# A decoder layer on one core: row factors spread over the partitions through DRAM in place of matmuls with ones, and the next half's work queued behind the residual adds

## The chip, the core and the metric

The kernel runs on one core of a Trainium2 chip. A core has a matrix engine (TensorE, here PE, with its weight loads as PEld), a vector engine (VectorE, DVE), an activation engine (ScalarE, ACT), a general engine (GpSimd, POOL) and a queue engine (SyncE, SP) that issues most transfers. Each runs its own list of instructions in order and waits on semaphores for the others. Tiles lie in an on-chip memory of 128 partitions; matmul results lie in banks of 128x512 f32. The metric is the device time of one execution in microseconds (us).

## What is computed

One layer of a decoder on 2048 tokens of width 1024, all in float32:

```python
xn = rms_norm(h, mix_norm_w)
q, f_logit, i_v, g, lru_x, lru_gate = split(xn @ w_in)      # 512 columns each
o_hg  = hgrn2_mix(q, f_logit, i_v, g, ...)   # gated linear recurrence, 4 heads, times silu(g)
o_lru = rglru_mix(lru_x, lru_gate, ...)      # conv, gates, linear recurrence, times gelu
h = h + concat(o_hg, o_lru) @ w_out
hn = rms_norm(h, ffn_norm_w)
h = h + (silu(gate) * up) @ w_down           # gate, up = split(hn @ w_gate_up)
return rms_norm(h, final_norm_w)

def rms_norm(x, w):
    return x * rsqrt(mean(x * x, axis=-1) + EPS) * w
```

What matters here is the first rms_norm: each token (a row of x) has one factor, rsqrt of its mean square.

## The kernel before

The tokens are worked on in two halves of 1024, each in two chunks of 512 (c = 0, 1) or eight row tiles of 128 (tt counts four of them in a chunk). A half goes through the input projection, the two mixers, the output projection, the FFN up and the FFN down. Every f32 matmul is done as three matmuls of split operands: a high part, rounded by ACT (L169 for weights, L233 for activations) or by a scaled copy, and a low part, the rest, subtracted by DVE (L170, L234). Names say which: whi_in and wlo_in are the input weights' parts, xn_c_00 and xn_c_01 the high parts of chunk c (first and last four of eight k slices), xn_c_10 and xn_c_11 the low parts.

**Row factors.** The Squares of x run on ACT with a sum along the row (L566 for half 0, L632 for half 1), DVE adds the parts (L558), POOL raises to the power -0.5 (L559). The result, ss_x, has a token's factor in a partition, 128 x 4 for a chunk. The projections of q, f and the rest need x with features in partitions and tokens along the row (tiles xk, 128 x 512), so the 512 factors must lie along the row, the same in all partitions. `row_spread` (L585) does this: for each of four row tiles DVE multiplies the identity by the factors (dgx, L590) and PE multiplies ones by it (tpbx, L591), which leaves the factors along the row in a bank. Half 0 multiplies xk by the bank (L598); half 1 copies the bank to a tile `row` on ACT (L639) and multiplies by that (L646).

In half 0 the first projection (v, `tok_wide`, L604) works on x without the factors and is scaled afterwards, in chunks pv_0 and pv_1; `row_spread` was called from its hook `between`, in the middle of its matmuls. Then come pa and pb (L261 to L263), which need xn.

**Half 1's preparation in half 0.** `norm_steps(c)` makes half 1's xn: `stat` (loads of x and the Squares), `spread`, and eight `apply` (load of xk, L646, the split). These steps are put into slots. `slot(i)` is called at eight places i = -4 to -1 of chunk 1's gate loop (after the Silu, L295, and the product with v, L1236) and at 28 places of the output projection's loop, after each residual add (L1303). Stats stand at slots -4 to 3, spreads at 8 and 9, applies at 12 to 27. In half 1 the same slots hold the FFN's first operands (act_a to act_g, from hn). A slot's code is only emitted there: the order on each engine is set by a scheduler that simulates a timeline and takes what it thinks is ready first. `tc.issue_after(ins)` adds an edge to that schedule: instructions emitted under it, on the engine of `ins`, come behind `ins`.

**The output projection** is seven products in the order p1, p2, p6, p5, p7, p3, p4 of sums of the mixers' outputs (operands mx_a to mx_g, made from hg, y and their sums s at L1224), into banks pox and poyp (L1298). DVE adds each bank to a tile res that holds x, and SP writes it to DRAM as h.

Of the kernel before, what the change touches and what calls it, by code (L numbers as in the profile page):

```python
# [8 lines left out]
F32 = mybir.dt.float32  # L9
F32R = mybir.dt.float32r  # L10
AF = mybir.ActivationFunctionType
ALU = mybir.AluOpType

P = 128
SEQ = 2048
D = 1024
KT = D // P
# [20 lines left out]
def hybrid_layer(ctx: ExitStack, tc: tile.TileContext, x, x_t, norm_w, cols, w_in, gate_w, w_out, w_gu, w_down, out):  # L38
# [26 lines left out]
    def late(nm):  # L65
        return sb.tile([P, CW], F32, tag="late", name=nm, bufs=5)
# [4 lines left out]
    def aux(nm):  # L71
        return psp.tile([P, CW], F32, tag="aux", name=nm)
# [25 lines left out]
    hst = const.tile([P, NU], F32, name="hst")  # L98
    nc.gpsimd.memset(hst, 0.0)
    v = nc.vector  # L100
    ones = const.tile([P, 1], F32, name="ones")
    nc.gpsimd.memset(ones, 1.0)
    tinies = const.tile([P, 17, 4], F32, name="tinies")
    n4 = [0]

# [456 lines left out]
    def row_factors(c, rows):  # L562
        sums = [small.tile([P, 4], F32, tag="ss", name=f"ss{n}_x0_{c}", bufs=8) for n in range(2)]
        for i, p in enumerate(rows):
            tt, n = divmod(i, 2)
            nc.scalar.activation(out=p, in_=p, func=AF.Square, scale=1.0 / 32.0, accum_out=sums[n][:, tt : tt + 1])  # L566
        return factor(sums, f"x0_{c}")
# [16 lines left out]

    def row_spread(c, rs, nm="x0"):  # L585
        nm = f"{nm}_{c}"
        pbc, dg = aux("tpb" + nm), late("dg" + nm)
        for tt in range(TPC):
            ts = slice(tt * P, (tt + 1) * P)
            v.tensor_scalar(out=dg[:, ts], in0=ident, scalar1=rs[:, tt : tt + 1], scalar2=None, op0=ALU.mult)  # L590
            nc.tensor.matmul(pbc[:, ts], lhsT=ones.broadcast_to([P, P]), rhs=dg[:, ts], start=True, stop=True)  # L591
        return pbc

    def normalised(c, xs, pbc):
        xn = act_tile(f"xn0_{c}")
# [5 lines left out]
                quarter.extend([ins, dve])  # L601
        return xn

    def tok_wide(w4, xt, nm, between):  # L604
        banks = [bank(f"{nm}_{tt}") for tt in range(TPC)]
        for k in range(KT):
            whi, wlo = w4[k // 2]
            ks = slice((k % 2) * CW, (k % 2 + 1) * CW)
            order = [(tt, i) for tt in range(TPC) for i in range(3)]
            if k == 0:  # L610
                order.sort(key=lambda o: (o[1], o[0]))
            for tt, i in order:
                w = (whi, whi, wlo)[i][:, ks]
                a = part(xt, int(i == 1), k, slice(tt * P, (tt + 1) * P))
                ins = nc.tensor.matmul(banks[tt], lhsT=a, rhs=w, start=(k + i == 0), stop=(k == KT - 1 and i == 2))  # L615
            if k in between:
                with tc.issue_after(ins.ins):
                    between[k]()
        return banks

    def norm_steps(c):
        box = {}
        sums = []

        def stat(tt):
            if tt == 0:
                sums.extend(small.tile([P, 4], F32, tag="ss", name=f"ss{n}_x1_{c}", bufs=8) for n in range(2))
            r0 = T + c * CW + tt * P
            for n in range(2):
                p = xin(f"x1_{c}_{tt}_{n}")  # L630
                nc.sync.dma_start(out=p, in_=x[r0 : r0 + P, n * CW : (n + 1) * CW])
                nc.scalar.activation(out=p, in_=p, func=AF.Square, scale=1.0 / 32.0, accum_out=sums[n][:, tt : tt + 1])  # L632
            if tt == TPC - 1:
                box["rs"] = factor(sums, f"x1_{c}")

        def spread():
            pbc = row_spread(c, box["rs"], "x1")
            box["row"] = late(f"row1_{c}")
            nc.scalar.copy(out=box["row"], in_=pbc)  # L639

        def apply(k):
            if k == 0:
                box["xn"] = act_tile(f"xn1_{c}")
            p = xin(f"xk1_{c}_{k}")
            nc.sync.dma_start(out=p, in_=x_t[k * P : (k + 1) * P, T + c * CW : T + (c + 1) * CW])
            v.scalar_tensor_tensor(  # L646
                out=p, in0=p, scalar=par[:, C_NW + k : C_NW + k + 1], in1=box["row"], op0=ALU.mult, op1=ALU.mult
            )
            split([part(box["xn"], s, k) for s in range(2)], p)

        return box, [lambda tt=tt: stat(tt) for tt in range(TPC)], spread, [lambda k=k: apply(k) for k in range(KT)]
# [442 lines left out]
    for half in range(2):  # L1094
# [12 lines left out]
        for c in range(NC):  # L1107
            if c == 0:
                wv = ws.take(4)
                vts = []  # L1110
            vt = block(f"v{half}_{c}", F32)
            vts.append(vt)
            if half == 0:
                def factors(c):
                    rows[c] = row_factors(c, acc[c])

                wide = []
                banks = tok_wide(wv, xw[c], f"pv0_{c}", {7 - 3 * c: lambda c=c: wide.append(row_spread(c, rs[c]))})
                for tt in range(TPC):
                    r = rs[c][:, tt : tt + 1]  # L1120
                    if tt % 2:
                        v.tensor_scalar(out=vt[:, tt, :], in0=banks[tt], scalar1=r, scalar2=None, op0=ALU.mult)
                    else:
                        nc.scalar.activation(out=vt[:, tt, :], in_=banks[tt], func=AF.Copy, scale=r)
                xt.append(normalised(c, xs[c], wide[0]))
                continue
            for tt in range(TPC):
                ps = tok_mm(wv, xt[c], tt, f"pv{half}_{c}_{tt}")
                nc.scalar.copy(out=vt[:, tt, :], in_=ps)
                later.pop(0)()  # L1130
# [80 lines left out]
        def slot(i):  # L1211
            for f_ in fill.pop(i, ()):
                f_()
# [13 lines left out]
        for c in range(NC):  # L1227
            for tt in range(TPC):
                ps = tok_mm(wg, xt[c], tt, f"pg{half}_{c}_{tt}")
                hook(32 + c * TPC + tt)  # L1230
                if lrus and (c, tt) == (0, 1):
                    exps()
                    ends()
                sg = page(f"sg{half}_{c}_{tt}")
                table_act(sg, ps, AF.Silu)
                v.tensor_tensor(out=vts[c][:, tt, :], in0=vts[c][:, tt, :], in1=sg, op=ALU.mult)  # L1236
                if c == 1:
                    slot(tt - 4)
            t = block(f"hg{half}_{c}", F32)
            hg.append(t)  # L1240
            for tt in range(TPC):
                tp = transposed(tt, 0, vts[c][:, tt, :], f"o{half}_{c}_{tt}")
                nc.scalar.activation(
                    out=t[:, :, tt * P : (tt + 1) * P], in_=tp, func=AF.Copy, scale=par[:, C_HN : C_HN + 1]
                )
            if c == 0:
                operand("p1", t)
                operand("p2", ys[0])
# [30 lines left out]
        for i, name in enumerate(OORDER):  # L1279
            wo = wos.take(2)  # L1280
            if i < 6:
                wos.ahead(2)
                prepare(OORDER[i + 1])
            if name in ("p2", "p5"):
                banks_y = [aux(f"poy{name}_{tt}_{half}") for tt in range(TPC)]
            banks = banks_y if name in ("p2", "p5", "p3") else banks_x
            first = name in ("p1", "p2", "p5")
            a = op.pop(name)
            c, n = to[name]
            if i in (1, 2, 5):  # L1290
                residual_in(*to[OORDER[i + 1]])
            for tt in range(TPC):
                tsl, ps = slice(tt * P, (tt + 1) * P), banks[tt]
                for q in range(4):
                    whi, wlo = (w[:, (q % 2) * CW : (q % 2 + 1) * CW] for w in wo[q // 2])
                    ahi, alo = (z[:, q, tsl] for z in a)
                    for m, (x_, y_) in enumerate(((ahi, whi), (ahi, wlo), (alo, whi))):
                        nc.tensor.matmul(  # L1298
                            ps, lhsT=x_, rhs=y_, start=first and q + m == 0, stop=q == 3 and m == 2, skip_group_check=not first
                        )  # L1300
                g = c * TPC + tt
                p = res[g, n]
                v.tensor_tensor(out=p, in0=p, in1=ps, op=ALU.add)  # L1303
                if name in ("p2", "p7", "p3", "p4"):
                    nc.sync.dma_start(out=h_d[half][g][n], in_=p)
                slot(4 * i + tt)
                if i == 6 and tt == 0:
                    if half == 0:
                        ws.ahead(4)
                    else:  # L1310
                        sums_start(0)
                        sums(0).make(0)
                        sums(0).done.add(0)
# [142 lines left out]
```

## Time and profile before

| | us |
|---|---|
| time, median of 3 runs (2073.08 to 2073.85) | 2073.59 |
| profiled execution | 2073.64 |
| its span, first to last instruction | 2071.6 |
| PE busy | 2059.0 |
| DVE busy | 1555.6 |
| ACT busy | 1014.7 |
| POOL busy | 73.7 |

A row of the timeline view gives a start, a duration, the engine, the line, the operation, out<-in, the shape and a count; rows of like instructions are merged, and in brackets stands how long the engine was idle just before and what ended that. A row of the view of transfers gives out<-in, the issuing queue, a count, the size and the median time from issue to landing. A row of the waits view has who waited for whom: total us, times, longest. Line numbers are those of the kernel before; after the change the same lines have numbers that are 1 to 11 lower.

### The profile page before, as it was taken

To read this page: it belongs to the slowest core of one execution; us is meant where nothing else is said; L and a number is where in the kernel's file an instruction comes from. 1 tells how busy PE (TensorE), PEld (TensorE's weight loads), DVE (VectorE), ACT (ScalarE), POOL (GpSimd) and SP (SyncE) were. 2 spreads that over 40 slices of the span, in tenths; PEclk is the share of its full clock that TensorE was granted. 3 is DMA by queue.
4 is the path that set the end of the run, shared out by engine and by line. 5 is a ranking of instruction groups with operands and counts; after the bars stand their busy time and mean duration, and the time that the engine had idled before them with its cause. 6 is when DMAs were issued, how large, how long until landed. Compare 5 with 4: busy or idle time off the path is not lost.

```text
span 2071.6 us, 26049 instructions
## 1 busy us (share of the span) xinstructions
PE 2059.0 (99%) x9570; PEld 1709.1 (83%) x9570; DVE 1555.6 (75%) x2509; ACT 1014.7 (49%) x1681; POOL 73.7 (4%) x105
## 2 busy tenths in 40 slices
PE   9999999999999999999999999999999999999998
PEld 8888887888888888888888888888888888888887
DVE  7878758836888599767667578779776676669787
ACT  7677776456777554343343344245333333344333
POOL 1011100000000000000000000001000000000000
PEclk9999999999999999999999999999999999999999
DMA  7322227841111264433433384346332232266424
GB/s 265 105 74 81 67 78 243 296 126 41 41 41 42 105 230 148 148 127 118 142 127 128 112 302 140 122 162 199 107 119 90 96 133 92 85 250 234 155 80 147
DMA packets 148351, 279.60 MB, mean 135 GB/s; under 512 B 12288, under 2 KB 28672, under 8 KB 148224
## 3 DMA queue, kind: packets, MB, share of 16 engines
q1 hardware_dynamic: 148080, 277.92, 39.5%
q8 instruction: 75, 1.23, 0.2%
q14 instruction: 52, 0.43, 0.1%
q10 hardware_dynamic: 144, 0.03, 0.0%
HBM read 210.53 MB, written 67.37 MB: 134 GB/s over the span
## 4 chain that ended last, share of the span: by engine, by line
PE 96%; ACT 1%; DVE 1%; DMA 1%; issue 0%; POOL 0%; DVEq 0%; POOLq 0%; ACTq 0%; SPq 0%
PE quad_e L771 12%; PE quad_g L771 12%; PE quad_a L771 12%; PE pda L1042 10%; PE pdb L1042 7%; PE quad_f L771 6%; PE pox L1298 4%; PE pa L261 3%; PE pb L262 3%; PE pa L263 3%; PE pb L263 3%; PE pa L262 3%; PE pb L261 3%; PE poyp L1298 3%; PE pv L615 2%; PE pd L910 1%
## 5 line engine op out<-in xcount | busy, mean ns | idle before, releaser
L771 PE MATMUL quad_e<-act_c,wgu_c 128*128 128x512 f32 x528 | 128.6, 390 | 0.0
L771 PE MATMUL quad_e<-act_e,wgu_e 128*128 128x512 f32 x528 | 127.5, 389 | 0.0
L771 PE MATMUL quad_f<-act_f,wgu_f 128*128 128x512 f32 x528 | 127.5, 389 | 0.0
L771 PE MATMUL quad_g<-act_g,wgu_g 128*128 128x512 f32 x528 | 127.5, 389 | 0.0
L771 PE MATMUL quad_a<-act_a,wgu_a 128*128 128x512 f32 x528 | 127.4, 389 | 0.0
L771 PE MATMUL quad_a<-act_b,wgu_b 128*128 128x512 f32 x528 | 127.1, 389 | 0.3 <-ACT e L808 0.3
L771 PE MATMUL quad_g<-act_d,wgu_d 128*128 128x512 f32 x528 | 127.2, 389 | 0.0
L771 PEld LDWEIGHTS quad_a<-act_b,wgu_b 128*128 128x128 f32 x528 | 99.1, 188 | 21.2 <-ACT e L808 0.6
L771 PEld LDWEIGHTS quad_a<-act_a,wgu_a 128*128 128x128 f32 x528 | 99.1, 188 | 20.8 <-ACT wgu_a L233 0.3
L771 PEld LDWEIGHTS quad_g<-act_g,wgu_g 128*128 128x128 f32 x528 | 99.1, 188 | 20.6
L771 PEld LDWEIGHTS quad_f<-act_f,wgu_f 128*128 128x128 f32 x528 | 99.1, 188 | 20.6
L771 PEld LDWEIGHTS quad_e<-act_e,wgu_e 128*128 128x128 f32 x528 | 99.1, 188 | 20.6
L771 PEld LDWEIGHTS quad_g<-act_d,wgu_d 128*128 128x128 f32 x528 | 99.1, 188 | 20.4
L771 PEld LDWEIGHTS quad_e<-act_c,wgu_c 128*128 128x128 f32 x528 | 99.1, 188 | 20.3
L655 DVE TENSOR_TENSOR u<-u,quad_g 128x512 f32<-128x512 f32 x88 | 60.3, 685 | 59.7 <-PE quad_g L771 59.6
L261 PE MATMUL pa<-xn,whi_in 128*128 128x512 f32 x256 | 100.9, 394 | 0.0
L263 PE MATMUL pa<-xn,whi_in 128*128 128x512 f32 x256 | 100.6, 393 | 0.0
L262 PE MATMUL pb<-xn,wlo_in 128*128 128x512 f32 x256 | 100.5, 393 | 0.0
L263 PE MATMUL pb<-xn,whi_in 128*128 128x512 f32 x256 | 100.5, 392 | 0.0
L262 PE MATMUL pa<-xn,wlo_in 128*128 128x512 f32 x256 | 100.4, 392 | 0.0
L261 PE MATMUL pb<-xn,whi_in 128*128 128x512 f32 x256 | 100.1, 391 | 0.0
L293 ACT ACT_TABLE_LOAD x74 | 94.9, 1283 | 2.5 <-PEq L1445 1.2
(375 smaller groups left out, 4883.8 us busy)
## 6 DMA issues: line engine op xcount, KB each, us to landing
raw<-in_w_gu SPq DMA_DIRECT2D x88, 512.0 KB, 3.8
raw_in<-in_w_in SPq DMA_DIRECT2D x47, 512.0 KB, 4.2
ao_p<-as SPq DMA_DIRECT2D x76, 256.0 KB, 2.5
xk<-in_x_t SPq DMA_DIRECT2D x32, 256.0 KB, 5.3
x<-in_x SPq DMA_DIRECT2D x32, 256.0 KB, 4.5
res<-in_x SPq DMA_DIRECT2D x32, 256.0 KB, 6.5
raw_o_p<-wo_p SPq DMA_DIRECT2D x16, 512.0 KB, 4.7
h<-res SPq DMA_DIRECT2D x32, 256.0 KB, 4.0
```

The source lines that it names most:

```text
L261: nc.tensor.matmul(ps, lhsT=whi[:, ks], rhs=hi, start=(k == 0), stop=False)
L262: nc.tensor.matmul(ps, lhsT=wlo[:, ks], rhs=hi, start=False, stop=False)
L263: nc.tensor.matmul(ps, lhsT=whi[:, ks], rhs=lo, start=False, stop=(k == KT - 1))
L293: in_line(lambda: nc.scalar.preload_act_table(func))
L615: ins = nc.tensor.matmul(banks[tt], lhsT=a, rhs=w, start=(k + i == 0), stop=(k == KT - 1 and i == 2))
L655: (e or v).tensor_tensor(out=out, in0=a, in1=b, op=op)
L771: nc.tensor.matmul(ps, lhsT=w[:, s, ks], rhs=x, start=first and k + n == 0, stop=k == 3 and n == 2, skip_group_check=not first)
L910: nc.tensor.matmul(ps, lhsT=a[:, 0, tsl], rhs=wlo[:, nsl], start=False, stop=False)
L1042: nc.tensor.matmul(ps, lhsT=x, rhs=y, start=first and q + n == 0, stop=q == gr.n - 1 and n == 2, skip_group_check=not first)
L1298: nc.tensor.matmul(ps, lhsT=x_, rhs=y_, start=first and q + m == 0, stop=q == 3 and m == 2, skip_group_check=not first)
```

## The change

```diff
     def row_spread(c, rs, nm="x0"):
         nm = f"{nm}_{c}"
-        pbc, dg = aux("tpb" + nm), late("dg" + nm)
-        for tt in range(TPC):
-            ts = slice(tt * P, (tt + 1) * P)
-            v.tensor_scalar(out=dg[:, ts], in0=ident, scalar1=rs[:, tt : tt + 1], scalar2=None, op0=ALU.mult)
-            nc.tensor.matmul(pbc[:, ts], lhsT=ones.broadcast_to([P, P]), rhs=dg[:, ts], start=True, stop=True)
-        return pbc
+        d = dram.tile([TPC, P], F32, name="rs_" + nm)
+        row = late("row" + nm)
+        nc.gpsimd.dma_start(out=d.rearrange("t p -> p t"), in_=rs)
+        nc.gpsimd.dma_start(out=row, in_=d.rearrange("t p -> (t p)").partition_broadcast(P))
+        return row
...
         def spread():
-            pbc = row_spread(c, box["rs"], "x1")
-            box["row"] = late(f"row1_{c}")
-            nc.scalar.copy(out=box["row"], in_=pbc)
+            box["row"] = row_spread(c, box["rs"], "x1")
...
             if half == 0:
...
-                wide = []
-                banks = tok_wide(wv, xw[c], f"pv0_{c}", {7 - 3 * c: lambda c=c: wide.append(row_spread(c, rs[c]))})
+                row = row_spread(c, rs[c])
+                banks = tok_wide(wv, xw[c], f"pv0_{c}")
...
                 if c == 1:
-                    slot(tt - 4)
+                    with tc.issue_after(at["last"]):
+                        slot(tt - 4)
...
-                v.tensor_tensor(out=p, in0=p, in1=ps, op=ALU.add)
+                add = v.tensor_tensor(out=p, in0=p, in1=ps, op=ALU.add)
...
-                slot(4 * i + tt)
+                with tc.issue_after(add.ins):
+                    slot(4 * i + tt)
```

The tile of ones and the hook `between` of `tok_wide` go too. `at["last"]` is the last ACT instruction that went through the table of functions, there the Silu of this tt, so the edge binds the slot's ACT instructions (the Squares of half 1's rows). The second edge binds the slot's DVE instructions. Neither binds a slot's transfers on SP or POOL; their places follow from the simulated timeline.

On DVE, at the start of half 0, before: the end of chunk 0's low parts, which stand behind its eight xk (a row names line, operation, out<-in and size; wlo_in_4 and _5 are the low parts of the weights of pa and pb, ss_x_1 the sum for chunk 1's factors):

```order
L234 TENSOR_TENSOR xn_0_11_462<-xk_0_4_184,xn_0_01_460 128x512
L234 TENSOR_TENSOR xn_0_11_462<-xk_0_5_185,xn_0_01_460 128x512
L234 TENSOR_TENSOR xn_0_11_462<-xk_0_6_186,xn_0_01_460 128x512
L170 TENSOR_TENSOR wlo_in_4_633<-raw_in_4_630,whi_in_4_632 128x1024
L234 TENSOR_TENSOR xn_0_11_462<-xk_0_7_187,xn_0_01_460 128x512
L558 SCALAR_TENSOR_TENSOR ss_x_1_341<-ss_x_1_331,ss_x_1_332 128x4
L170 TENSOR_TENSOR wlo_in_5_639<-raw_in_5_636,whi_in_5_638 128x1024
```

After, behind the first projection's v_0 and ahead of the eight xk of chunk 0 (rowx_0 is the row that the DMA brings):

```order
L1111 TENSOR_SCALAR v_0_342<-pv_0_1_348,ss_x_0_306 128x512
L1111 TENSOR_SCALAR v_0_342<-pv_0_3_350,ss_x_0_306 128x512
L168 TENSOR_TENSOR wlo_in_4_619<-raw_in_4_616,whi_in_4_618 128x1024
L556 SCALAR_TENSOR_TENSOR ss_x_1_339<-ss_x_1_329,ss_x_1_330 128x4
L595 SCALAR_TENSOR_TENSOR xk_0_0_178<-xk_0_0_178,par,rowx_0_344 128x512
```

and some rows later, in chunk 0's low parts:

```order
L595 SCALAR_TENSOR_TENSOR xk_1_2_188<-xk_1_2_188,par,rowx_1_481 128x512
L595 SCALAR_TENSOR_TENSOR xk_1_3_189<-xk_1_3_189,par,rowx_1_481 128x512
L232 TENSOR_TENSOR xn_0_11_454<-xk_0_4_182,xn_0_01_452 128x512
L232 TENSOR_TENSOR xn_0_11_454<-xk_0_5_183,xn_0_01_452 128x512
L595 SCALAR_TENSOR_TENSOR xk_1_4_190<-xk_1_4_190,par,rowx_1_481 128x512
L595 SCALAR_TENSOR_TENSOR xk_1_5_191<-xk_1_5_191,par,rowx_1_481 128x512
L232 TENSOR_TENSOR xn_0_11_454<-xk_0_6_184,xn_0_01_452 128x512
```

The sum of chunk 1 and the weight's low part moved ahead of chunk 0's xk, and chunk 1's xk, which need its row, now stand between the low parts of chunk 0.

On ACT, where chunk 1's gate ends in half 0, before (hg_1 is scaled in four pieces from tp_o_1_0 to tp_o_1_3; whi_o_p are output weights, x_1 rows of half 1):

```order
L1243 ACTIVATE hg_1_3017<-tp_o_1_1_0_3024,par 128x4x128
L169 CAST whi_o_p_0_3068<-raw_o_p_0_3066 128x1024
L1243 ACTIVATE hg_1_3017<-tp_o_1_2_0_3030,par 128x4x128
L169 CAST whi_o_p_1_3074<-raw_o_p_1_3072 128x1024
L169 CAST whi_o_p_0_3161<-raw_o_p_0_3159 128x1024
L1243 ACTIVATE hg_1_3017<-tp_o_1_3_0_3036,par 128x4x128
```

and after:

```order
L1233 ACTIVATE hg_1_3003<-tp_o_1_1_0_3010,par 128x4x128
L167 CAST whi_o_p_1_3060<-raw_o_p_1_3058 128x1024
L626 ACTIVATE x_1_0_0_3079,ss_x_1_3077<-x_1_0_0_3079 128x512
L626 ACTIVATE x_1_0_1_3082,ss_x_1_3078<-x_1_0_1_3082 128x512
L1233 ACTIVATE hg_1_3003<-tp_o_1_2_0_3016,par 128x4x128
L626 ACTIVATE x_1_1_0_3098,ss_x_1_3077<-x_1_1_0_3098 128x512
L626 ACTIVATE x_1_1_1_3101,ss_x_1_3078<-x_1_1_1_3101 128x512
L1233 ACTIVATE hg_1_3003<-tp_o_1_3_0_3022,par 128x4x128
```

Squares of half 1's rows took the place of two weight casts between the pieces of hg_1.

On DVE, between the two low parts of mx_f in half 0, after (before, two adds stood there, and no mx_g):

```order
L232 TENSOR_TENSOR mx_f_0_3164<-s_0_3158,mx_f_0_3163 128x1024
L1293 TENSOR_TENSOR res_0_0_3028<-res_0_0_3028,poyp_0_0_3169 128x512
L232 TENSOR_TENSOR mx_e_0_3250<-s_0_3157,mx_e_0_3249 128x1024
L1213 TENSOR_TENSOR y_0_662<-y_0_662,s_0_3158 128x1024
L232 TENSOR_TENSOR mx_e_0_3250<-s_0_3157,mx_e_0_3249 128x1024
L1293 TENSOR_TENSOR res_1_0_3030<-res_1_0_3030,poyp_1_0_3170 128x512
L232 TENSOR_TENSOR mx_g_0_3340<-hg_1_3003,mx_g_0_3339 128x1024
L1293 TENSOR_TENSOR res_2_0_3032<-res_2_0_3032,poyp_2_0_3171 128x512
L232 TENSOR_TENSOR mx_f_0_3164<-s_0_3158,mx_f_0_3163 128x1024
```

Seven instructions stand between the two mx_f rows.

More of the change, by code (lines that the diff above doesn't have):

```diff
@@ L100, in hybrid_layer @@
     v = nc.vector
-    ones = const.tile([P, 1], F32, name="ones")
-    nc.gpsimd.memset(ones, 1.0)
     tinies = const.tile([P, 17, 4], F32, name="tinies")
@@ L602, in normalised, with tok_wide @@
         return xn
-    def tok_wide(w4, xt, nm, between):
+    def tok_wide(w4, xt, nm):
         banks = [bank(f"{nm}_{tt}") for tt in range(TPC)]
@@ L614, in tok_wide @@
                 a = part(xt, int(i == 1), k, slice(tt * P, (tt + 1) * P))
[L615 to L618, printed above, removed]
+                nc.tensor.matmul(banks[tt], lhsT=a, rhs=w, start=(k + i == 0), stop=(k == KT - 1 and i == 2))
         return banks
@@ L1113, in hybrid_layer @@
             if half == 0:
-                def factors(c):
-                    rows[c] = row_factors(c, acc[c])
-                wide = []
-                banks = tok_wide(wv, xw[c], f"pv0_{c}", {7 - 3 * c: lambda c=c: wide.append(row_spread(c, rs[c]))})
+                row = row_spread(c, rs[c])
+                banks = tok_wide(wv, xw[c], f"pv0_{c}")
                 for tt in range(TPC):
@@ L1124, in hybrid_layer @@
                         nc.scalar.activation(out=vt[:, tt, :], in_=banks[tt], func=AF.Copy, scale=r)
-                xt.append(normalised(c, xs[c], wide[0]))
+                xt.append(normalised(c, xs[c], row))
                 continue
```

## Prediction

> **What bounds the kernel now.** I read the page's busy list first, then the waits of TensorE (PE) alone, then the lines that the change touches.
>
> ```profile
> PE 2059.0 (99%) x9570; PEld 1709.1 (83%) x9570; DVE 1555.6 (75%) x2509; ACT 1014.7 (49%) x1681; POOL 73.7 (4%) x105
> ```
>
> PE is busy for 2059.0 of a span of 2071.6 us. The profiled execution took 2073.64 us, so 2.04 us lie around its span; the median of the three runs is 2073.59. All below is summed against 2073.64, and 0.05 us of difference to the median is not worth carrying. The list of what PE waited for is short:
>
> ```profile
> PE warm L544 <- DVE warm L541: 1.5, 1, 1.5
> PE tpbx L591 <- DVE dgx L590: 1.4, 1, 1.4
> PE pox L1298 <- DVE mx_f L234: 1.2, 1, 1.2
> PE pg L273 <- ACT sg L295: 0.8, 1, 0.8
> PE quad_a L771 <- ACT e L808: 0.3, 1, 0.3
> ```
>
> So the time is PE's work, and an edit is worth what it takes off PE's queue or out of this list. The second row is a line that the change deletes. Everything on the other engines counts only if it comes too late for PE.
>
> **The matmuls that go.** The spread of row factors is L591, sixteen matmuls in four groups, recorded twice each:
>
> ```profile
> L591 PE MATMUL tpbx<-dgx,ones x32: 271/275/376, 28.0 to 358.8; 128*128 128x128 f32 x32
> 27.32 0.62 PE L615 MATMUL pv<-whi_in,xw 128*128 128x512 f32 x2
> 27.77 0.39 PE L615 MATMUL pv<-wlo_in,xw 128*128 128x512 f32 x1
> 28.00 1.05 PE L591 MATMUL tpbx<-dgx,ones 128*128 128x128 f32 x8
> 28.81 0.71 PE L615 MATMUL pv<-whi_in,xw 128*128 128x512 f32 x2
> 29.36 0.39 PE L615 MATMUL pv<-wlo_in,xw 128*128 128x512 f32 x1
> ...
> 354.04 0.49 PE L591 MATMUL tpbx<-dgx,ones 128*128 128x128 f32 x2 [1.39 <-DVE dgx L590]
> ```
>
> Three projection matmuls take 28.00 - 27.32 = 0.68 us, 0.227 each. With a group of eight in front, the next three start at 28.00 and end their turn at 29.36 + 0.23 = 29.59: 1.59 us, of which 0.68 are theirs. A group costs PE **0.91 us**, not the 1.05 of its row, since its end overlaps. Four groups: **3.64 us**. In the preparation of half 1 one group also has a wait of 1.39 us (last row), the 1.4 of the list; with no dgx there is nothing to wait for. Together **5.03 us**, if nothing new is late. The VectorE (DVE) and ScalarE (ACT) sides, 16 dgx instructions and two row copies, are off PE's path and count only in the queues below.
>
> **What the two DMAs cost: start of half 0.** Each spread becomes, on the POOL queue, a write of 512 factors of 4 bytes to DRAM and a read of 256 KB that repeats them over 128 partitions; the read waits for the write. Call L the time from the end of POOL's power to the landed row. No DMA is issued from POOL in this trace, so L is bounded by the nearest rows:
>
> ```profile
> wo_p<-wt SPq DMA_DIRECT2D x16, 256.0 KB, 2.6
> wfin<-in_norm_w SPq DMA_DIRECT2D x4, 512.0 KB, 4.5
> wffn<-in_norm_w SPq DMA_DIRECT2D x2, 512.0 KB, 5.9
> par<-in_cols ACTq DMA_DIRECT2D x1, 26.5 KB, 4.2
> res<-in_x SPq DMA_DIRECT2D x32, 256.0 KB, 6.5
> hd<-h SPq DMA_DIRECT2D x32, 256.0 KB, 8.5
> ```
>
> wo_p is a write to DRAM, wfin and wffn are reads repeated over the partitions, par is a load of short lines, one for each of 128 partitions, res and hd are the slower loads of the row's own size. Lower end: 2.6 + 4.5 = 7.1 us. Upper end: if time goes with the number of pieces, the write has four times par's, 16.8, plus 5.9 makes 22.7 us. I take 9 (par's 4.2 + wfin's 4.5, rounded up), because the row nearest to the write in kind, many short pieces, is par.
>
> What stands behind the row? Chunk 0:
>
> ```profile
> 21.75 1.02 POOL L559 TENSOR_TENSOR ss_x<-ss_x,tinies 128x4 f32<-128x4 f32 x1 [16.63 <-DVE ss_x L558]
> 41.56 1.95 POOL L559 TENSOR_TENSOR ss_x<-ss_x,tinies 128x4 f32<-128x4 f32 x1 [18.79 <-DVE ss_x L558]
> 29.75 5.35 DVE L598 SCALAR_TENSOR_TENSOR xk<-xk,par,tpbx 128x512 f32<-128x512 f32 x8
> 41.34 0.15 DVE L558 SCALAR_TENSOR_TENSOR ss_x<-ss_x,ss_x 128x4 f32<-128x4 f32 x1
> 35.17 2.49 DVE L234 TENSOR_TENSOR xn<-xk,xn 128x512 fp32r<-128x512 f32 x4
> 28.43 1.41 DVE L1122 TENSOR_SCALAR v<-pv,ss_x 128x512 f32<-128x512 f32 x2
> 383.14 1.41 DVE L646 SCALAR_TENSOR_TENSOR xk<-xk,par,row 128x512 f32<-128x512 f32 x2
> 51.62 0.39 PE L261 MATMUL pa<-xn,whi_in 128*128 128x512 f32 x1
> ```
>
> The factor is ready at 21.75 + 1.02 = 22.8. PE first needs chunk 0's split xn at the first pa, now 51.62 - 1.82 = 49.8. Between row and pa lie on DVE eight xk (5.35), a weight split (1.2) and one xn (0.6), so the row may land at 42: L up to 19 is hidden. Chunk 1 is tighter. Its sum (41.34 before) moves ahead of the eight xk, so its power starts near 36.3 and is done near 38.8. Behind the row DVE has eight xk, four xn of chunk 0, two v and the first xn of chunk 1: 5.35 + 2.49 + 1.41 + 0.6 = 9.9. PE needs that xn 52 matmuls after its first pa: 49.8 + 52 x 0.227 = 61.6. The row must land by 51.7, so **L up to 12.9 costs nothing, and each us beyond it costs PE one**. At 9, nothing; at the lower end nothing; at the upper end 9.8 us. The POOL queue holds nothing behind these DMAs that is wanted before. In the preparation of half 1 chunk 1's factors follow the second mx_f part (347.8 below), so are ready near 350, and its first xk, 383.14 before, comes some 28 us later even when it moves up by 5: beyond the upper end.
>
> The Trainium skill, "DMA: Bandwidth & Descriptors", section "Anatomy of one DMA — SWDGE (gpsimd) path", fits such a transfer with 2.0 us plus its bytes over 436 KB per us: as an estimate from that page, 2.0 + 2.6 = 4.6 us for L, below my lower end, and the sum would be the same. The same skill speaks against the change elsewhere: "SBUF — State Buffer", section "SBUF: two separate sides", says that descriptors of a POOL-issued DMA cannot be written while VectorE runs an operation that takes both shared ports. No run here shows such a DMA yet. I weigh the mechanism below as a rival.
>
> **What moves: half 0's output projection.** The next half's DVE work now stands behind the residual adds, the Squares of its rows behind the gate's Silu on ACT. PE's wait for mx_f is where this decides.
>
> ```profile
> 328.01 1.05 ACT L169 CAST whi_o_p<-raw_o_p 128x1024 fp32r<-128x1024 f32 x1 [2.18 <-DMA raw_o_p<-wo_p]
> 328.96 0.68 ACT L1243 ACTIVATE hg<-tp_o,par 128x512 f32<-128x512 f32 x1
> 329.68 1.23 DVE L1224 TENSOR_TENSOR s<-hg,y 128x1024 f32<-128x1024 f32 x1 [1.78 <-ACT hg L1243]
> 341.70 1.22 DVE L234 TENSOR_TENSOR mx_f<-s,mx_f 128x1024 fp32r<-128x1024 f32 x1
> 342.83 0.68 DVE L1303 TENSOR_TENSOR res<-res,poyp 128x512 f32<-128x512 f32 x1
> 347.43 1.22 DVE L234 TENSOR_TENSOR mx_f<-s,mx_f 128x1024 fp32r<-128x1024 f32 x1
> 342.97 0.73 PE L1298 MATMUL pox<-whi_o_p,mx_f 128*128 128x512 f32 x2 [1.20 <-DVE mx_f L234]
> x<-in_x SPq DMA_DIRECT2D x16, 256.0 KB, 3.1
> ```
>
> DVE's chain to mx_f starts with s, which waits for the last hg on ACT, and that stood behind a cast that waited 2.18 us for its weights. Now hg stands behind two Squares instead, whose rows (3.1 us to land) are loaded once Squares before them free their buffers. I put s at 327.7, 2.0 us earlier. From s to the first low part of mx_f stand twelve instructions, ten wide ones that follow each other at 1.14 us and two adds at 0.6 (a row's duration overlaps the next by 0.08): 12.6 us, so done near 340.3. PE would want it at 342.97 - 1.20 - 1.82 - 0.91 = 339.0. The wait stays: 1.3 for 1.2. The **second low part** is new. PE reaches it 27 matmuls later, 6.1 us, at 346.4. On DVE seven instructions now stand between the two, three residual adds and four wide ones: with its own 1.14 that is 7.5 us, so 347.8, against 5.7 before (342.83 to 347.43 + 1.14). **PE waits 1.4 us there.** From outside: if Squares and rows come together late, with loads of 6.5 us like res's in place of 3.1, both waits grow by 3.4; if hg comes as soon as DVE is free, 326.6, the first falls to 0.2.
>
> **Half 1's output projection and the first quads** have the FFN's operands queued behind the adds in the same way.
>
> ```profile
> 745.00:770.00 25.00, 25.00 (x112) 20.71 (x111) 25.00 (x35) 10.50 (x14) 0.00 (x0) 1.00 0.72 235
> 794.96 0.50 PE L771 MATMUL quad_a<-act_b,wgu_b 128*128 128x512 f32 x1 [0.32 <-ACT e L808]
> ```
>
> In that stretch DVE (third pair) is as full as PE, yet PE waits for nothing. No instruction is added, the last act splits needed by the first quads end some 4 to 6 us ahead in the new order, counted with 0.6 each. I cost this at 0, between -0.3 (the wait in the second row) and +2.
>
> **Sum.** 2073.64 - 3.64 - 1.39 + 0.1 + 1.4 = **2070.1 us**.
>
> **Rivals.** *All of it is gained*: the second mx_f wait does not come, because hg and s run earlier than I place them or DVE overtakes PE. For it: the cast with its 2.18 us of waiting is out of hg's way. Against: the seven instructions. 2073.64 - 5.03 = 2068.6, or 2067.4 if the first wait goes too.
>
> *Given back in the queues*: the late Squares hold hg_1_3, s and both mx_f parts, or an act split misses its quad. That adds 2 to 4 us: 2072.5 to 2075.
>
> *The slow row (slower)*: one mechanism at one place, chunk 1 at the start of half 0. Beyond L = 12.9 us, PE stalls 1:1 at the first xn of chunk 1. The gain is gone at L = 16.4, and the kernel is measurably slower from L = 20.5. At the upper end, 22.7, it takes 2079.9. For it: 512 single words, two transfers in a chain, a path never seen here. Against: no row of this size above hd's 8.5 us.
>
> *Held off by DVE*: if POOL cannot write descriptors while DVE works, chunk 1's write starts only when DVE's run of xk and splits ends, near 46.8, in place of 38.8, and the row is 8 us later: L of 17 and 2074.2. For it: DVE is busy without a gap there. Against: what it runs are operations with two tensors, the dgx with one are deleted. The Trainium skill's "SBUF — State Buffer" (section "Who interferes with whom") exempts two-input operations from holding the write side, and calls that inferred; by it this rival falls away.
>
> **How the numbers follow.** The forecast's own case, 2069.0 to 2072.5, has 0.38; all gained, 2066.8 to 2069.4, 0.28; given back 0.18; held off by DVE 0.05; slow row beyond L = 16 0.11. A run of this kernel tells about 0.2% from no change, 4.15 us: faster is below 2069.4, slower above 2077.7. Faster: 0.28 and 0.10 from the forecast's lower edge, 0.38. Slower: most of the slow row, 0.10, and 0.02 of mishaps in the queues. Same: 0.50. The range 2066.8 to 2077.0 leaves out about 0.05 below and 0.13 above.
>
> **What would show it.** In the profile after: no L591 row and PE's first pa near 49.8; PE's list without the dgx row, with mx_f at about 1.3 and 1.4; the rows of the two POOL DMAs and whether the eight xk of chunk 1 idle for a DMA, and how long; a PE wait at the first pa or pb of chunk 1 would be the slow row. s near 327.7 confirms the ACT step. A new PE wait outside these places, or one at the first quads, would make the forecast wrong.

## The result, and the profile after

| | before | after |
|---|---|---|
| time, median of 4 runs each | 2073.34 us | 2097.76 us |
| lowest to highest | 2072.85 to 2073.85 | 2095.05 to 2098.22 |
| profiled execution | 2073.64 us | 2098.22 us |
| its span | 2071.6 us | 2096.5 us |

The ratio is 1.0116, with a 95% interval of 1.0103 to 1.0128: the change makes the kernel 24.4 us slower. The prediction was 2070.1 us, with a range of 2066.8 to 2077.0. Where the experiments below give one time for a kernel, it is one run; 21 runs of the kernel before on one chip lie between 2072.43 and 2074.23 us, so a difference of 1 or 2 us between two single runs says little.

I read the profile after in the same order as before: the busy list, PE's waits, then the lines of the change. The first line of the busy list:

```profile
PE 2066.1 (99%) x9538; PEld 1711.2 (82%) x9538; DVE 1551.9 (74%) x2493; ACT 1015.3 (48%) x1681; POOL 77.4 (4%) x112
```

There are 32 fewer records on PE, the deleted matmuls, and yet PE is busy 7.1 us longer. The span grew by 24.9, so PE idles 17.8 us more (2096.5 - 2066.1 = 30.4, against 12.6). Both have to be explained: the idle time and the slower matmuls.

PE's waits (who for whom, total us, times, longest) say where it idles:

```profile
PE pa L261 <- DVE xn L232: 6.6, 1, 6.6
PE pr L467 <- ACT zb L458: 2.8, 1, 2.8
PE pa L259 <- ACT sf L293: 2.3, 2, 2.0
PE pox L1288 <- ACT mx_f L231: 2.2, 1, 2.2
PE quad_e L763 <- DVE res L1293: 1.9, 1, 1.9
...
PE pg L271 <- ACT sg L293: 1.5, 1, 1.5
```

The wait for dgx is gone, as it had to be. In its place stands a list of new ones, most of them in half 0 and in the preparation of half 1. The longest is at the start of half 0, where the prediction put its slow row; which operand PE waits for there is read below.

**The start of half 0.** The POOL timeline shows the two spreads (rs_x<-ss_x is the write to DRAM, rowx<-rs_x the read):

```profile
22.95 0.94 POOL L587 DMA_DIRECT2D rs_x<-ss_x  x1 [0.30 <-POOL ss_x L557]
35.91 0.57 POOL L588 DMA_DIRECT2D rowx<-rs_x  x1 [12.02 <-DMA rs_x<-ss_x]
43.62 1.49 POOL L557 TENSOR_TENSOR ss_x<-ss_x,tinies 128x4 f32<-128x4 f32 x1 [7.15 <-DVE ss_x L556]
45.52 0.81 POOL L587 DMA_DIRECT2D rs_x<-ss_x  x1 [0.41 <-POOL ss_x L557]
55.96 0.56 POOL L588 DMA_DIRECT2D rowx<-rs_x  x1 [9.62 <-DMA rs_x<-ss_x]
```

POOL waits 12.0 and 9.6 us for writes of 2 KB. The view of transfers (size, median us from issue to landing) has all four spreads:

```profile
rowx<-rs_x POOLq DMA_DIRECT2D x4, 256.0 KB, 6.2
...
rs_x<-ss_x POOLq DMA_DIRECT2D x4, 2.0 KB, 11.3
```

The small write is the slow one, not the read of 128 times its size. What it does to DVE and PE shows in the timeline:

```profile
43.37 0.16 DVE L556 SCALAR_TENSOR_TENSOR ss_x<-ss_x,ss_x 128x4 f32<-128x4 f32 x1 [5.34 <-ACT x L564]
50.14 0.49 PE L259 MATMUL pa<-xn,whi_in 128*128 128x512 f32 x1
56.56 0.39 PE L260 MATMUL pb<-xn,wlo_in 128*128 128x512 f32 x1
60.12 2.74 DVE L595 SCALAR_TENSOR_TENSOR xk<-xk,par,rowx 128x512 f32<-128x512 f32 x4 [7.59 <-DMA rowx<-rs_x]
62.78 1.29 DVE L232 TENSOR_TENSOR xn<-xk,xn 128x512 fp32r<-128x512 f32 x2
63.52 0.80 PE L261 MATMUL pa<-xn,whi_in 128*128 128x512 f32 x1 [6.57 <-DVE xn L232]
```

PE's first pa comes at 50.14, 1.48 earlier than before: chunk 0's row was hidden. Chunk 1's row is the problem, but what PE waits for is an operand of chunk 0. On DVE the last four low parts of chunk 0 stand behind the first four xk of chunk 1, as the order after the change shows (xn_0_11 behind xk_1_3). PE needs the first of them, at L261, after 28 matmuls of chunk 0; it has run dry at 56.95, while DVE stands idle for chunk 1's row. Behind the row DVE needs 3.4 us for four xk and this low part (60.12 to 63.52), so the row had to be there by 53.55, and it is late by the 6.57 us that PE waits. It is late for two reasons. It takes 60.1 - 45.1 = 15.0 us from power to landed row. And its sum itself is late: 43.37 in place of 36.3, because ACT had no rows to square:

```profile
37.13 0.63 ACT L564 ACTIVATE x<-x 128x512 f32<-128x512 f32 x1 [7.35 <-DMA x<-in_x]
```

**The write holds up other transfers.** The view of transfers for 20 to 45 us, after and then before:

```profile
x<-in_x SPq DMA_DIRECT2D x8, 256.0 KB, 13.0
```

```profile
x<-in_x SPq DMA_DIRECT2D x8, 256.0 KB, 6.6
```

Loads issued on SP's queue take 13.0 us in place of 6.6 while POOL's write is out. One window of that time (busy us of PE, PEld, DVE, ACT and POOL; the last three columns are PE's clock, the DMA engines' share, GB/s), after and then before:

```profile
28.00:32.00 4.00, 4.00 (x19) 3.32 (x18) 1.42 (x3) 1.64 (x2) 0.00 (x0) 1.00 1.50 91
```

```profile
28.00:32.00 4.00, 4.00 (x23) 3.46 (x22) 4.00 (x7) 3.62 (x8) 0.00 (x0) 1.00 1.04 393
```

From 28 to 32 us the DMA engines move 91 GB/s where they moved 393, at no smaller share of busy time, and ACT (fourth pair) runs dry for want of rows. DVE (third pair) has little to do as well, but that is not the loads' doing: in the run with whole lines below, where they are on time, it is busy for 1.36 us of these 4.

**The clock.** The other part of the loss, the slower matmuls, stands in the clock column of these windows of after:

```profile
57.99:61.40 3.41, 0.00 (x0) 0.00 (x0) 1.28 (x2) 0.49 (x1) 0.00 (x0) 1.00 0.29 87
61.40:68.23 6.83, 4.71 (x11) 3.75 (x12) 6.83 (x12) 5.10 (x9) 0.00 (x0) 0.50 0.00 0
...
259.36:262.78 3.42, 1.45 (x7) 0.89 (x6) 3.42 (x13) 3.37 (x6) 0.00 (x0) 1.00 0.00 0
262.78:266.20 3.42, 3.42 (x10) 2.68 (x9) 3.42 (x6) 2.97 (x3) 0.30 (x1) 0.50 0.02 5
...
358.35:361.77 3.42, 1.47 (x6) 0.67 (x4) 3.42 (x4) 2.96 (x6) 0.00 (x0) 1.00 1.02 387
361.77:368.60 6.83, 6.15 (x15) 4.81 (x16) 6.83 (x9) 3.03 (x5) 0.82 (x1) 0.50 1.00 322
```

After each of these stretches of 3.41 us in which PE was idle for 57% or more, the granted clock is 0.50 for one or two such stretches. Half of PE's busy time there is lost: (4.71 + 3.42 + 6.15) / 2 = **7.1 us**. Before, no such stretch lies between PE's start and its end.

The account: 17.8 us more idle, 7.1 at half clock, less 3.64 of deleted matmuls makes 21.3 of the span's 24.9. The rest, 3.6 us, is spread over matmuls that I could not place one by one.

### The profile page after: what moved, and what is told of

Read it like the earlier page. It is cut to its first block, busy times and chain, and to the rows that moved or that the text cites. A ratio compares the mean times of both kernels' runs of the same rounds, so it can differ in the third digit from the quotient of the medians.

```text
span 2096.5 us, 26003 instructions
## 1 busy us (share of the span) xinstructions
PE 2066.1 (99%) x9538; PEld 1711.2 (82%) x9538; DVE 1551.9 (74%) x2493; ACT 1015.3 (48%) x1681; POOL 77.4 (4%) x112
## 4 chain that ended last, share of the span: by engine, by line
PE 84%; DVE 6%; DMA 6%; ACT 3%; issue 1%; SPq 0%; POOL 0%; DVEq 0%; POOLq 0%; ACTq 0%
PE quad_e L763 11%; PE quad_g L763 11%; PE quad_a L763 11%; PE pda L1034 10%; PE pdb L1034 7%; PE quad_f L763 6%; PE pa L259 2%; PE pb L261 2%; PE pb L259 2%; PE pb L260 2%; PE pa L260 2%; PE pa L261 2%; PE pox L1288 2%; DMA raw_o_p<-wo_p 2%; PE pg L271 1%; PE pg L272 1%
## 5 line engine op out<-in xcount | busy, mean ns | idle before, releaser
L261 PE MATMUL pa<-xn,whi_in 128*128 128x512 f32 x256 | 102.3, 399 | 6.6 <-DVE xn L232 6.6
L259 PE MATMUL pa<-xn,whi_in 128*128 128x512 f32 x256 | 102.2, 399 | 2.3 <-ACT sf L293 2.3
L261 PE MATMUL pb<-xn,whi_in 128*128 128x512 f32 x256 | 100.8, 394 | 0.0
L259 PE MATMUL pb<-xn,whi_in 128*128 128x512 f32 x256 | 100.8, 394 | 0.0
```

Of the source, the lines that this page charges most:

```text
L259: nc.tensor.matmul(ps, lhsT=whi[:, ks], rhs=hi, start=(k == 0), stop=False)
L261: nc.tensor.matmul(ps, lhsT=whi[:, ks], rhs=lo, start=False, stop=(k == KT - 1))
```

## The experiments

**Theories.** (A) The scattered write is slow, and through it the rows and other loads are late. (B) The two edges put the work of DVE and ACT in a bad order. (C) POOL's queue is what is slow, or DVE holds it off. Each run below stands beside a run of the kernel before on the same chip.

**The edges alone.** The kernel before, with the two edges and no DMA:

```diff
-                    slot(tt - 4)
+                    with tc.issue_after(at["last"]):
+                        slot(tt - 4)
...
-                slot(4 * i + tt)
+                with tc.issue_after(add.ins):
+                    slot(4 * i + tt)
```

> Only the two edges are kept; the row factors are spread by dgx and matmuls with ones as before. Theory (the scattered write of 512 words holds up every other transfer of the core for about 8 us, and the waits behind it are the loss): no such write is left, so 2070 to 2077 us, no window with high DMA share and little moved. Rival (the edges and the new order are the loss): 2085 us or more.

Measured: 2073.92 us against 2073.42. PE's waits:

```profile
PE pox L1299 <- DVE res L1304: 1.6, 1, 1.6
PE quad_e L771 <- DVE res L1304: 1.5, 1, 1.5
```

The waits for mx_f and dgx, 1.2 and 1.4 before, are both gone, and two new ones of the same size stand behind residual adds. By one run the edges are worth nothing either way; B is not the cause.

**The DMAs alone.** The changed kernel with both edges taken out (the diff above, reversed).

> Only the two DMAs are kept; the slots carry no edges, as before. Theory (the scattered write holds up the transfers): 2088 to 2102 us, with the writes landing 10 us or more after their issue. Rival (edges): 2066 to 2074 us.

Measured: 2101.67 us against 2073.42, with a median of 10.6 us for the writes and the same wait at L261 (6.3 us). The loss is the DMAs'. With the edges beside them the kernel takes 2097.76; whether they help there, one run does not say.

**Another queue.** The write and the read go out on SP in place of POOL:

```diff
-        nc.gpsimd.dma_start(out=d.rearrange("t p -> p t"), in_=rs)
-        nc.gpsimd.dma_start(out=row, in_=...)
+        nc.sync.dma_start(out=d.rearrange("t p -> p t"), in_=rs)
+        nc.sync.dma_start(out=row, in_=...)
```

> As the changed kernel, but SP issues the write and the read of the row in place of POOL. Theory (many small pieces): the write still takes 8 us or more and other loads beside it still land late; 2085 us or more, since SP also waits in order for the write. Rival (it is the POOL queue, whatever it carries): the write takes 3 to 5 us, loads beside it land on time, 2066 to 2078 us.

Measured: 2097.04 us against 2073.42. The first two writes in the view of transfers, with a weight load issued 1.6 us before the second, in two windows:

```profile
rs_x<-ss_x SPq DMA_DIRECT2D x1, 2.0 KB, 8.0
raw_in<-in_w_in SPq DMA_DIRECT2D x1, 512.0 KB, 11.6
rs_x<-ss_x SPq DMA_DIRECT2D x1, 2.0 KB, 11.1
```

The same write is as slow from SP, so C falls in both its forms: neither POOL's queue nor DVE holding POOL off is needed for a slow write. The load beside it suffers here too, 11.6 us where the kernel before has 5.4 for its kind in this part. But the loss is not the same chain of waits. SP issues the first write only at 30.40, behind the loads of x, which land on time (6.2 us). Here ACT waits 4.8 us for the weight load that the second write holds up, and PE's longest wait, 5.3 us at L259, ends behind ACT. That the totals agree within 1 us is chance as far as these runs show.

**Whole lines.** The changed kernel without edges; PE transposes the 128 x 4 factors to 4 x 128 and ACT copies them, so the write takes four lines of 512 bytes:

```diff
+        tp, flat = aux("tpr" + nm), small.tile([TPC, P], F32, ...)
+        nc.tensor.transpose(out=tp[:TPC, :P], in_=rs, identity=ident)
+        nc.scalar.copy(out=flat, in_=tp[:TPC, :P])
-        nc.gpsimd.dma_start(out=d.rearrange("t p -> p t"), in_=rs)
+        nc.gpsimd.dma_start(out=d, in_=flat)
```

> As the changed kernel, still from POOL, but PE first transposes the 128 x 4 factors and ACT copies them out, so that the write is 4 lines of 512 bytes instead of 512 words. Theory (many small pieces): the write lands in 2 to 5 us, no other load is held up, 2067 to 2075 us. Rival (POOL queue): as slow as the changed kernel, 2088 us or more.

Measured: 2073.28 us against 2073.42, with the write in the view of transfers:

```profile
rs_x<-flat_x POOLq DMA_DIRECT2D x4, 2.0 KB, 3.9
```

The same 2 KB, on the same queue, at the same place in the program, land in 3.9 us in place of 10.6, and 28.4 us of the loss are gone (2101.67 to 2073.28). The loads beside it are on time as well: for 20 to 45 us the loads of x have a median of 6.2 us, 11.8 with the scattered write and the same lack of edges. From 28 to 32 us, with the write of whole lines out since 28.21, the DMA engines move 410 GB/s, and ACT is busy for 3.83 us of the 4. No stretch at half clock is left between PE's start and its end. What remains is that the deleted matmuls still bring nothing: PE's first pg of half 0 comes at 263.06, 260.89 before. Ahead of it PE has 16 records of the deleted matmuls less, two transposes more and three new waits, 0.7, 0.8 and 1.0 us, none of them for a row. That they come from the rows' latency at the start of half 0 is likely, but not shown.

**Probes.** What about the write is slow? The kernel before with seven transfers that nobody reads, one by one in half 1's FFN:

```diff
+        d = dram.tile([TPC, P], F32, ...)
+        pool.dma_start(out=d.rearrange("t p -> p t"), in_=ss)
...
+        d = dram.tile([P, TPC], F32, ...)
+        pool.dma_start(out=d, in_=ss)
...
+        d = dram.tile([TPC, P, P], F32, ...)
+        pool.dma_start(out=d[:, :, 0].rearrange("t p -> p t"), in_=ss)
```

> The kernel before, with one transfer added behind each of seven row tiles' factors in half 1's FFN, whose results nothing reads: 512 words packed in 2 KB from POOL (as in the change), 128 pieces of 16 bytes, 512 words each in a 512-byte line of its own, 512 packed words from SP, 128 packed words, 512 words read back from DRAM, 256 packed words. Theory A (cost by the number of pieces, at some 15 ns each): about 8 us for each 512-word write wherever the words lie, 2 to 4 us for 128 pieces and 128 words, 5 to 6 us for 256. Theory B (words that share a line of memory wait for each other): 512 words in lines of their own take 2 to 4 us, the packed ones about 8. The weight loads in flight beside a slow one land late by about its length, those beside a fast one on time. The read back: 2 to 4 us if only writes are slow.

In order of time, each from the view of transfers around it: the change's write; 128 pieces of 16 bytes; 512 words 512 bytes apart; the change's write from SP; 128 packed words; the 512 words read back; 256 packed words:

```profile
probe<-ss_hs POOLq DMA_DIRECT2D x1, 2.0 KB, 8.8
probe<-ss_hs POOLq DMA_DIRECT2D x1, 2.0 KB, 1.8
probe<-ss_hs POOLq DMA_DIRECT2D x1, 2.0 KB, 2.2
probe<-ss_hs SPq DMA_DIRECT2D x1, 2.0 KB, 10.5
probe<-ss_hs POOLq DMA_DIRECT2D x1, 0.5 KB, 7.8
back<-probe POOLq DMA_DIRECT2D x1, 2.0 KB, 2.6
probe<-ss_hs POOLq DMA_DIRECT2D x1, 1.0 KB, 7.9
```

The number of pieces is not the price: 512 words far apart take 2.2 us, 128 words side by side 7.8. Nor is it the read of such words, 2.6. It is the write of single words that lie side by side in DRAM.

The probes also show what a slow write does to loads, away from the crowd of half 0. Two loads of hn that SP issues while the 128 words are out (window 1000 to 1006), and the same two in the kernel before:

```profile
hn<-hths SPq DMA_DIRECT2D x2, 256.0 KB, 5.5
```

```profile
hn<-hths SPq DMA_DIRECT2D x2, 256.0 KB, 2.5
```

It is so beside all four slow writes, the one from SP included: their hn loads take 5.3 to 6.9 us. The fast writes have landed before their hn loads go out, and these take 2.3 to 3.2, with 2.3 to 2.8 in the kernel before. Weight loads issued some 2 us ahead of a slow write are on time. PE waits for none of these loads: the time did not move, 2073.54 us against 2074.10.

**One half at a time.** Both with the edges; in the first only half 0's spreads are scattered DMAs and half 1's stay matmuls, in the second the reverse. Both use the change's two DMAs word for word:

```diff
-                banks = tok_wide(wv, xw[c], f"pv0_{c}", {7 - 3 * c: lambda c=c: wide.append(row_spread(c, rs[c]))})
+                wide = [row_dma(c, rs[c], "x0")]
+                banks = tok_wide(wv, xw[c], f"pv0_{c}", {})
```

```diff
-            pbc = row_spread(c, box["rs"], "x1")
-            box["row"] = late(f"row1_{c}")
-            nc.scalar.copy(out=box["row"], in_=pbc)
+            box["row"] = row_dma(c, box["rs"], "x1")
```

> Edges as in the change; the scattered write and the read of the row only in half 0, matmuls with ones in half 1's preparation. Theory: the stall at the first operands of half 0, the waits that follow it and the slow clock behind it are there in full, 2087 to 2093 us, and nothing in half 0's output projection beyond 2 us. Rival (the loss at the start is the new order, not the write): 2074 to 2080 us.

> Edges as in the change; the scattered write only in half 1's preparation. Theory: two writes hold up the output weights, 4 to 9 us more than before less 1.8 us of matmuls, 2076 to 2081 us, with waits for mx_f or the weights' parts in the output projection. Rival (rows with 28 us to spare cost nothing): 2070 to 2073 us.

Measured against 2074.10: 2094.05 us for half 0 alone, 20.0 slower and 1 us above the expected range; 2077.16 for half 1 alone, 3.1 slower. The two add up to 23.0 of the change's 24.4. In half 0 alone PE waits at the same place (4.5 us), and the clock follows:

```profile
59.98:63.39 3.41, 0.00 (x0) 0.00 (x0) 3.05 (x5) 2.13 (x4) 0.00 (x0) 1.00 0.00 0
63.39:66.80 3.41, 3.07 (x7) 2.49 (x8) 3.41 (x7) 2.12 (x4) 0.00 (x0) 0.50 0.00 0
```

**Keep what pays.** Half 0 with its matmuls; half 1's preparation with the transposed write, which has the longer cover. First with both edges, then with none, then with the second edge in half 0 only (the first edge stays):

```diff
+                if half == 0:
+                    with tc.issue_after(add.ins):
+                        slot(4 * i + tt)
+                else:
+                    slot(4 * i + tt)
```

> Edges as in the change; half 0 keeps the matmuls; in half 1's preparation PE transposes the factors and four lines of 512 bytes are written and read back. Theory (nothing is held up, two groups of ones less, 1.82 us, and two short transposes more): 2070.5 to 2073 us. Rival (what PE saves comes back as other waits): 2073 to 2076 us.

> As the run with transposed factors in half 1's preparation, but without the two edges. If the edges cost nothing and gain nothing: the same time within 2 us, 2069 to 2072, with PE's wait at the first quads back to 0.3 us and a wait for mx_f of about 1 us. If the edges are what makes the output projection free of waits: 2072 to 2075 us.

> As the run with transposed factors in half 1's preparation, with the edge behind the residual add in half 0 alone. PE's wait of 1.4 us at the first quad_e is gone or 0.3 us: 2068 to 2070.5 us, about 0.2% faster than before. Rival (the wait comes from elsewhere): 2070 us and the wait is still there.

Measured: with both edges 2070.01 us against 2074.10 (one run each), 0.5 below the expected range. Without edges 2070.43 against 2073.41 (10 and 21 runs), ratio 0.9986, interval 0.9977 to 0.9995. With the edge in half 0 only **2068.68** against 2073.41 (11 and 21 runs), ratio 0.9980, interval 0.9971 to 0.9988. This one beats both kernels; all that PE waits for in it:

```profile
PE warm L544 <- DVE warm L541: 1.5, 1, 1.5
PE pg L273 <- ACT sg L295: 0.8, 1, 0.8
PE quad_a L780 <- ACT e L817: 0.3, 1, 0.3
```

The dgx wait and the mx_f wait are gone and nothing took their place. Without any edge the mx_f wait stays (1.5 us); with the edge in half 1 too, quad_e waits 1.4.

**How far apart.** The kernel before with seven writes of 512 words, the words 8, 16, 32, 64, 128 and 256 bytes apart, then side by side; nobody reads them:

```diff
+        step = (2, 4, 8, 16, 32, 64, 1)[g]
+        d = dram.tile([TPC, P, step], F32, ...)
+        nc.gpsimd.dma_start(out=d[:, :, 0].rearrange("t p -> p t"), in_=ss)
```

> The kernel before, with seven writes of 512 words from POOL in half 1's FFN that nothing reads, the words 8, 16, 32, 64, 128 and 256 bytes apart and then packed. If words in one 512-byte line wait for each other: 8 to 9 us for packed words, and about half for each doubling of the distance until the fixed part of some 2 us is left, 5 us at 8 bytes, under 3 at 64. If the grain is 64 bytes: about 8 us until 32 bytes apart, 2 to 3 us from 64 on.

The first, the second and the last, from the view of transfers around each:

```profile
probe<-ss_hs POOLq DMA_DIRECT2D x1, 2.0 KB, 4.1
probe<-ss_hs POOLq DMA_DIRECT2D x1, 2.0 KB, 2.2
probe<-ss_hs POOLq DMA_DIRECT2D x1, 2.0 KB, 10.3
```

At 8 bytes 4.1 us, at 16 bytes 2.2, and so (2.2 to 2.5) at every larger distance; at 4 bytes 10.3. Neither lines of 512 bytes nor grains of 64 explain that: words 16 bytes apart share both and are fast.

**Apart, in place.** The changed kernel with its words 16 bytes apart; the rest of the tile is zeroed by a write from SP first:

```diff
-        d = dram.tile([TPC, P], F32, name="rs_" + nm)
+        d = dram.tile([TPC, P, 4], F32, name="rs_" + nm)
+        nc.sync.dma_start(out=d.rearrange("t p w -> p t w"), in_=zero4)
...
-        nc.gpsimd.dma_start(out=d.rearrange("t p -> p t"), in_=rs)
+        nc.gpsimd.dma_start(out=d[:, :, 0].rearrange("t p -> p t"), in_=rs)
```

> The changed kernel with one thing varied: the words of the four scattered writes lie 16 bytes apart in DRAM instead of 4. Queue, order, both edges, number of pieces and number of writes stay. The row is read from the tile's first 512 words, so it holds only 128 factors and zeros between. If the distance of the words is what makes the change slow, the writes land in 2 to 5 us, the half-clock stretches at half 0's first pa and first pg go, and the time is 2071 to 2077 us, near that of e4_transposed. If any write from 128 partitions with one word each in these places costs this much, whatever the distance, they land in 8 us or more and the time stays at 2088 us or above.

Measured: 2079.83 us against 2073.65, between the two expectations. The writes:

```profile
rs_x<-zero SPq DMA_DIRECT2D x4, 8.0 KB, 7.9
rs_x<-ss_x POOLq DMA_DIRECT2D x4, 2.0 KB, 5.8
```

The wait of 6.6 us at L261 is gone from PE's list. The distance takes the write from 11.3 us to 5.8 and the loss from 24 us to 6, so it is the larger part of the price. How much of the rest belongs to scattered words in a crowded place, and how much to the zero writes, which I added and which take 7.9 us themselves, this run cannot tell. Of the three falls of the clock one is left.

## Why the prediction was wrong

**The matmuls: right.** L591 is gone, and PE's first pa came 1.48 us earlier where the prediction had 1.82 (pv starts 0.10 later, 6.24 for 6.14). The wait for dgx is gone with it.

**Chunk 0's row: right, with luck.** The prediction hid L up to 19. It was 19.0 (22.65 to the row's landing near 41.6), more than twice the 9 that it reckoned with, and PE's first pa waited for nothing.

**L, and what the write does to other loads: these are the steps that failed.** The prediction took 9 us for L, by par's row for the write and wfin's for the read; its measure for chunk 1 is 15.0, past the point of 12.9 from which it said PE pays. The read was about as thought (median 6.2, 4.1 here). The write took 9.8 to 14 us where par's row has 4.2. par is a load of lines of its own per partition, not a write of single words side by side, and the probes show that this, not the number of pieces, sets the price. The upper end, 22.7, came from a count of pieces, a reason that the probes refute, though it did contain the value. The estimate from the Trainium skill, 4.6 us for L by "DMA: Bandwidth & Descriptors", section "Anatomy of one DMA — SWDGE (gpsimd) path", was further off: the write alone has a median of 11.3. For the transposed write its 2.0 us plus bytes comes nearer, against 3.9 measured.

The second step is a term that the prediction left at nothing: no part of it asked what the new transfer does to those beside it. It let chunk 1's power end at 38.8. It ended at 45.1, 6.3 us later, since the rows that it sums were loaded beside chunk 0's write.

**The slow row was the right rival, with 0.11, but its place and its price were wrong.** It named the first xn of chunk 1, 52 matmuls after PE's first pa, and so a limit of 51.7 for the row. What PE waited for is a low part of chunk 0, after 28 matmuls, and the limit is 53.55. The prediction had these four low parts in its sum behind the row, but did not ask when PE needs them. The rule itself, one us of PE for each us beyond the limit, holds there. By the forecast the row lands at 47.8 (38.8 + 9), 5.75 us ahead of that limit; it came 12.3 us later, 6.0 by L and 6.3 by the late power, and PE waited 6.6. Either alone would have cost PE under 1 us at this place (an estimate from these numbers). Two things came on top, for which the rival had no price:

- *The clock.* A wait that empties most of a 3.41-us stretch also halves the clock after it: 7.1 us in all. The Trainium skill, "TensorE: Matmul & The Clock Gate", section "What's actually happening", puts the fall to half rate after one idle window of about 3.4 us. The lengths of the stretches agree; but here a stretch with 1.47 us of work in 3.42 was enough.
- *What comes later.* In half 0 pr waits 2.8 us for zb, pa 2.3 for sf, pg 1.5 for sg, none of which touches a row factor. The run with half 0's spreads alone has these waits (2.3, 4.4 and 1.4) and the run with half 1's alone only pg's 0.8, as before: they follow from half 0's start. By which queue each came to be late stays open.

**Held off by DVE: right to give it little.** From SP, whose transfers POOL does not issue, the write is as slow (8.0 to 11.1 us).

**Half 1's preparation: wrong.** The prediction saw chunk 1's row 28 us ahead of its use, beyond the upper end. For the row that holds. But the output weights loaded beside the writes came late. Two of them, issued at 335.45 and 336.09 as chunk 0's write went out (336.75), landed after 15 us, where the version with whole lines has 6.7 in the same two us:

```profile
raw_o_p<-wo_p SPq DMA_DIRECT2D x2, 512.0 KB, 15.0
350.43 2.00 ACT L167 CAST whi_o_p<-raw_o_p 128x1024 fp32r<-128x1024 f32 x2 [7.70 <-DMA raw_o_p<-wo_p]
```

ACT waits 7.7 us for them, mx_f is late and PE waits 2.2 at L1288, with half clock behind it (358.35 in the windows above). With the transposed write in the same place there is no such wait, and the time is 7.15 us lower (2077.16 to 2070.01).

**The edges: size right, places half right.** Predicted were 1.3 and 1.4 at the two mx_f parts, and 0 (up to 2) at the first quads. The edges alone gave no mx_f wait, 1.6 behind a residual add at PE's first matmul with mx_g, and 1.5 at quad_e: 3.1 in all, 2.7 predicted. s came at 326.1 rather than 327.7, so mx_f was early, as the rival "all gained" had it. What came late in DVE's queue is the add itself: PE goes on when it has ended, and the low part of mx_g had been done 3.6 us before (348.56 against 352.17). The wait for dgx, which the prediction put down as the DMAs' gain, went with the edges alone too. The first quads were within their bound, at the wrong end.

**Without the write's price** the range of the forecast would have held: the version with whole lines in half 1 and half 0's matmuls kept takes 2070.01 with both edges. That this is the forecast's 2070.1 is partly luck: it still has half of the matmuls and is spared the slow rows, so it tests the edges and half 1's gain, not half 0's. With whole lines in both halves, and no edges, the time is 2073.28.

## What to carry to other kernels

Turn a factor per partition into whole lines (here one small transpose) before it goes to DRAM: 512 words side by side cost more than 256 KB read back. When a new transfer has no row in the trace, ask what it does to the transfers beside it as well as how long it takes. Where an engine runs its queue in order, look for what stands behind the operand that may be late, and when each of these is needed: here the operand of another chunk. And price a wait of PE by the clock as well: one that fills 57% or more of a 3.41-us stretch cost up to 3.1 us more behind it here.

## What the runs showed of the hardware

- Writes to DRAM of single 4-byte words: side by side 7.8 us (128 words), 7.9 (256), 8.8 to 10.3 (512, in the FFN), 9.0 to 14 (512, at the change's places, over all runs); 8 bytes apart 4.1; 16 bytes and more 2.2 to 2.5, all in the FFN (16 bytes at the change's places 3.5 to 7.4). From SP 8.0 to 11.1. Only the distance was varied; what in the memory or the queue makes neighbours slow stays open.
- While such a write is out, loads issued beside it land late: beside a write from POOL 13.0 us for 6.6 on SP's queue, with 91 GB/s moved where 393 were, and in the FFN 5.3 to 5.6 for 2.3 to 2.8; beside a write from SP 11.6 for 5.4, and in the FFN 6.4 to 6.9. Beside the same 2 KB as whole lines they are on time (6.2).
- PE's granted clock goes to 0.50 on a grid of 3.41 us, after a stretch that was idle for 57% (1.95 of 3.42) or more; over all runs no stretch with 52% or less did that (1.75 and 1.78 of 3.41 in the run with half 0's spreads alone). It came back after one to three stretches (three in the run of the DMAs alone, 342.13 to 352.37).
